# Four projections through the 512-column form, in halves of 256 output channels

## The chip, the cores and the metric

The kernel runs on one core of a Trainium2 chip. The metric is device time in microseconds (us), the median of repeated executions. Five engines work side by side, each through its own instructions in order: TensorE (PE, matmuls, with its weight loads PEld), VectorE (DVE), ScalarE (ACT), GpSimd (POOL) and SyncE (SP, here the queue that issues most loads).

## What is computed

One layer that mixes four branches: a gated linear recurrence, dilated window attention, an RWKV-7 recurrence and a convolution. All start from one product with a wide weight matrix (T is 256 tokens, D_MODEL 2048, D_IN 18048):

```
h = jnp.einsum('bsd,de->bse', x, w_in) + b_in
(a_x, a_gate, q, k, v, b_gate, c_r, c_k, c_v, c_wd, c_ad, c_gate,
 d_val, d_glu, d_gate, merge_logits) = jnp.split(h, split_points, axis=-1)
...
for n in range(N_BRANCH):
    mixed = mixed + merge_g[:, :, n] * jnp.einsum('bsc,cd->bsd', ys[n] * jax.nn.silu(gates[n]), w_br[n])
out = jnp.einsum('bsd,de->bse', mixed, w_out)
return _layernorm(ALPHA * x + out, ln_g, ln_b)
```

q and k have 1536 channels each and are read in three strips of 512; every gate has 512. The change touches four such strips of `w_in`: the gate of branch c, the first of q, the last of k, and the gate of branch b.

## The kernel before

**Precision.** Every factor of a large product is kept as a rounded part and a remainder: x as `xh` and `xl`, side by side in one tile `x2` (per row block 256 columns of `xh`, then 256 of `xl`), and the weights as `wh` (an ACT cast, L219) and `wl` (a DVE subtraction, shown at L65, which is the line of the wrapper through which all DVE work goes). A product is the sum of wh·xh, wh·xl and wl·xh, three matmuls.

**The two forms of a projection.** `proj` (L330, through `channel_major` and `multiply`, L240) gives 512 channels as four blocks of 128, each 256 columns wide, two blocks to a PSUM bank, so two banks for the whole projection; each of its 192 matmuls moves 256 columns. `wide` (L256) takes a whole bank for each block of 128 channels, moves `xh` and `xl` together as one operand of 512 columns against `wh` (L270), and `wl` against `xh` alone (L273); the two halves of the bank are added when the bank is emptied. It takes four banks: from the pool `pss` (four banks, the stream's) or from `psb` (four banks, shared with the recurrences and the attention). Of the six strips of q and k the four in the middle go through `wide`, the first of q (Q0 below) and the last of k (K2) through `proj`.

**What empties a bank.** For Q0 and K2 one ACT pass per block adds the bias (L977). For the gates, `silu_gate` (L333), one ACT sigmoid (L338) and one DVE pass per block. The gate of branch c is `gc`; it is then multiplied by `yc`, the result of the RWKV branch, and split into `ych` and `ycl` (`gated`, L342).

**What runs beside it.** The recurrences and the attention are generators that `pump` advances between weight pieces. Their DVE instructions are pinned behind everything already traced on DVE; the rest is placed by a scheduler that orders each engine's instructions before the run; splits of weights have a raised priority. The RWKV generator ends, for each of four chunks of 64 steps, with a chain: `bks` (DVE), transposes `pbk` (PE), `pu` (PE), `us` (DVE), `psa` (PE), `sv` (DVE copies), `pst` (PE), `sv` (DVE sums) and the next chunk's `pu`; after the last chunk `py` (PE), `wy` and its square `sq` (ACT), `psvar` (PE), `sel` (ACT square root), a reciprocal and two small splits into `selr` (DVE), `psvar` again (PE), then `wy` (DVE) and `yc` (DVE). In the program's text all of that is ahead of `gc` (`finish(yc)`, L966); on the engines the scheduler lays the matmuls of `gc` and Q0 between its steps.

**Rotation.** Tiles of one tag take turns: `pss` has 4 banks, `wh` and `wl` three buffers each, `raw` (the landed weights) four, `mg` two. A tile's first writer waits for the last reader of the tile that had the buffer.

Of the kernel before, what the change touches and what calls it, by code (L numbers as in the profile page):

```python
# [11 lines left out]
F32 = mybir.dt.float32  # L12
F32R = mybir.dt.float32r
AF = mybir.ActivationFunctionType
ALU = mybir.AluOpType
# [4 lines left out]
P = 128  # L20
T = 256
DM = 2048
KT = DM // P
KP = 2
BW = 512
NJ = BW // P
# [8 lines left out]
C_AX, C_AG, C_Q, C_K, C_V, C_BG = 0, 512, 1024, 2560, 4096, 5632  # L35
C_R, C_CK, C_CV, C_WA, C_CG = 6144, 6656, 7168, 7680, 7808
# [37 lines left out]
def tile_hybrid(  # L74
# [4 lines left out]
    S, G, PE = nc.scalar, nc.gpsimd, nc.tensor  # L79
    V = Paced(tc, nc.vector)  # L80
# [6 lines left out]
    bp = ctx.enter_context(tc.tile_pool(name="bp", bufs=1))  # L87
    pss = ctx.enter_context(tc.tile_pool(name="pss", bufs=4, space=PSUM))
# [3 lines left out]
    def big(tag, bufs, name, dt=F32):  # L92
        pool = ap if tag in ("mx4", "tt") else xp if tag in ("yh", "yl") else bp
        return pool.tile([P, NJ, T], dt, tag=tag, name=name, bufs=bufs)

    def tt(name, dt=F32):
        return big("tt", 5, name, dt)
# [4 lines left out]
    def ra(name, shape, dt=F32):  # L102
        return bp.tile(shape, dt, tag="ra", name=name, bufs=6)

    def bank(name):
        return psb.tile([P, 512], F32, tag="pb", name=name)
# [8 lines left out]
    x2 = xp.tile([P, KT, 2, T], F32R, tag="x2", name="x2")  # L115
    xh, xl = x2[:, :, 0, :], x2[:, :, 1, :]
# [5 lines left out]
    def load_x(k, n):  # L122
        xs = rk("xs")[:, 0:n, :]
        load(xs, xr[:, k : k + n, :])
        return xs

    def split_x(xs, k, n):
        V.tensor_copy(xh[:, k : k + n, :], xs)
        V.tensor_tensor(xl[:, k : k + n, :], xs, xh[:, k : k + n, :].bitcast(F32), op=ALU.subtract)
# [47 lines left out]
    def bcol(c):  # L177
        return bc[:, c // P : c // P + 1]
# [5 lines left out]
    def pump(budget):  # L184
        V.side = True
        credit[0] = min(credit[0], 0.0) + budget
        while side and credit[0] > 0:
            try:
                cost = next(side[0])
                credit[0] -= cost  # L190
            except StopIteration:
                side.popleft()
        V.side = False
# [9 lines left out]
    def fetch(src, c0, n, k, nk, queue=None):  # L203

        if nk == 1:
            raw = rk("raw1").rearrange("p a b -> p (a b)")[:, 0:n].rearrange("p (k n) -> p k n", k=1)
        else:
            raw = rp.tile([P, nk, n], F32, tag="raw", name="raw", bufs=4)
        ins = (queue or nc.sync).dma_start(raw, src[:, k : k + nk, c0 : c0 + n])
        if queue:  # L210
            tc.keep_in_program_order(ins)
        return raw

    def split(src, c0, n, k, nk, raw=None):
        raw = raw or fetch(src, c0, n, k, nk)
        h = wp.tile([P, nk, n], F32R, tag="wh", name="wh", bufs=3)
        l = wp.tile([P, nk, n], F32R, tag="wl", name="wl", bufs=3)
        with tc.high_priority(offset=AHEAD):
            S.copy(h, raw)  # L219
            V.tensor_tensor(l, raw, h.bitcast(F32), op=ALU.subtract)  # L220
        return h, l

    def pieces(nk, n):
        kn = KP * 512 // n
        return [(k, kn) for k in range(0, nk, kn)]

    w_in_r = w_in.rearrange("(k p) c -> p k c", p=P)
# [3 lines left out]
    def columns(n):  # L231
        ps = [pss.tile([P, 2, T], F32, tag="ps", name="ps") for _ in range((n // P + 1) // 2)]
        return [ps[j // 2][:, j % 2, :] for j in range(n // P)]

    def multiply(ps, h, l, k0, kn, nk, rh, rl, j0=0):
        for j in range(j0, len(ps)):
            for k in range(kn):
                kk = k0 + k
                for i, (w, r) in enumerate(((h, rh), (h, rl), (l, rh))):
                    PE.matmul(  # L240
                        ps[j],
                        w[:, k, (j - j0) * P : (j - j0 + 1) * P],
                        r[:, kk, :],
                        start=(kk == 0 and i == 0 and j % 2 == 0),
                        stop=(kk == nk - 1 and i == 2),
                        skip_group_check=True,
                    )
# [8 lines left out]
    def wide(c0, stream):  # L256

        ps = [pss.tile([P, 512], F32, tag="ps", name="ps") if stream else bank("psq") for _ in range(NJ)]
        for k0, kn in pieces(KT, 512):
            raw = fetch(w_in_r, c0, 512, k0, kn)  # L260
            h = [ra("wa", [P, 512], F32R) for _ in range(kn)]
            l = wp.tile([P, kn, 512], F32R, tag="wl", name="wl", bufs=3)
            with tc.high_priority(offset=AHEAD):
                for k in range(kn):
                    S.copy(h[k], raw[:, k, :])  # L265
                    V.tensor_tensor(l[:, k, :], raw[:, k, :], h[k].bitcast(F32), op=ALU.subtract)
            for j in range(NJ):
                for k in range(kn):
                    both = x2[:, k0 + k, :, :].rearrange("p a t -> p (a t)")
                    PE.matmul(ps[j], h[k][:, j * P : (j + 1) * P], both, start=(k0 + k == 0), stop=False, skip_group_check=True)  # L270
            for j in range(NJ):
                for k in range(kn):
                    PE.matmul(  # L273
                        ps[j][:, T:], l[:, k, j * P : (j + 1) * P], xh[:, k0 + k, :], start=False,
                        stop=(k0 + k == KT - 1), skip_group_check=True,
                    )
            pump(BUD)
        return ps

    def opening(cols, budget):  # L280

        pss_ = [columns(512) for _ in cols]
        todo = []
        for k0, kn in ((0, 1), (1, 1)) + tuple((k, KP) for k in range(2, KT, KP)):
            todo += [(k0, kn, n, q, T if k0 == 0 and n == 0 else 512) for n in range(2) for q in range(2 if k0 == 0 and n == 0 else 1)]

        def get(k0, kn, n, q, w):
            xs = load_x(k0, kn) if n == 0 and q == 0 else None
            return xs, fetch(w_in_r, cols[n] + q * w, w, k0, kn, S if kn == 1 and n == 0 else nc.sync)

        got = [get(*p) for p in todo[:5]]
        for i, (k0, kn, n, q, w) in enumerate(todo):
            if i >= len(got):
                got.append(get(*todo[i]))
            xs, raw = got[i]
            h, l = split(w_in_r, 0, w, k0, kn, raw)
            if xs is not None:
                split_x(xs, k0, kn)
            multiply(pss_[n][0 : 2 * q + w // P], h, l, k0, kn, KT, xh, xl, 2 * q)
            if n:  # L300
                pump(budget * kn)
        return pss_
# [25 lines left out]
    BUD = 1300.0  # L328

    def proj(c0, n=512):  # L330
        return channel_major(w_in_r, KT, c0, n, xh, xl, BUD)

    def silu_gate(c0, name):  # L333
        ps = proj(c0)
        g = tt(name)
        for j in range(NJ):
            b = bcol(c0 + j * P)
            S.activation(g[:, j, :], ps[j], AF.Sigmoid, bias=b)  # L338
            V.scalar_tensor_tensor(g[:, j, :], ps[j], b, g[:, j, :], op0=ALU.add, op1=ALU.mult)
        return g  # L340

    def gated(y, g, name):  # L342
# [593 lines left out]
    ps, pd = opening((C_AX, C_DL), BUD)  # L936
# [4 lines left out]
    ps = proj(C_DV)  # L941
# [7 lines left out]
    ps = proj(C_WA, 128)  # L949
# [14 lines left out]
    yhd = gated(yd[0], gd, "yd")  # L964
    merge(3, *yhd, False, False)
    finish(yc)  # L966
    gc = silu_gate(C_CG, "gc")
    yhc = gated(yc[0], gc, "yc")

    qk = []  # L970
    for i in range(6):
        c0 = C_Q + i * 512
        t = rk("qt" if i < 3 else "kt")
        pairs = 0 < i < 5
        ps = wide(c0, i % 2) if pairs else proj(c0)
        for j in range(NJ):
            S.activation(t[:, j, :], ps[j][:, T:] if pairs else ps[j], AF.Identity, bias=bcol(c0 + j * P))  # L977
            if pairs:
                V.tensor_tensor(t[:, j, :], t[:, j, :], ps[j][:, 0:T], op=ALU.add)
        qk.append(t)  # L980
    qt, kt = qk[0:3], qk[3:6]
    vt = []
    for g in range(3):
        bv = ra("bv", [P, 512])
        G.dma_start(bv, row(b_row[C_V + g * 512 : C_V + (g + 1) * 512]))
        ps = token_major(w_in_r, KT, C_V + g * 512, *by_token(xh, xl), BUD)
        t = rk("vt").rearrange("p a b -> p (a b)").rearrange("p (t n) -> p t n", t=2)
# [2 lines left out]
        vt.append(t)  # L990
    hb = bias_tiles()
    side.append(attention(qt, kt, vt, hb, yb))
    gb = silu_gate(C_BG, "gb")
    merge(2, *yhc, False, False)
    finish(yb)
    yhb = gated(yb[0], gb, "yb")
# [85 lines left out]
    for i, (c0, n) in enumerate(((0, 512), (512, 512), (1024, 512), (1536, 256))):  # L1082
        ps = token_major(w_out_r, KT, c0, mix(0), mix(1), BUD, n)
# [10 lines left out]
    for t in range(2):  # L1094
        ps = pss.tile([P, 512], F32, tag="ps", name="ps")
# [92 lines left out]
```

## Time and profile before

| | |
|---|---|
| median of 3 runs | 1047.32 us (1047.31 to 1048.41) |
| the profiled execution's own time | 1049.88 us |
| its span on the core | 1048.1 us |
| PE busy | 1039.7 us, 99% of the span |
| DVE, ACT busy | 729.3 us (70%), 501.2 us (48%) |
| granted TensorE clock, mean | 0.996 |

The rows come from one profiled execution; times in them are counted from the start of its span. A matmul in fp32 of small size shows as two records, and the ends of matmuls are modelled, so a row's duration runs a little past the start of the next one: the pace of a row of matmuls is read from start to start, or from the chain of waits, which gives each stretch without overlap. "Idle" is time in which an engine waited, and the name behind the arrow is what it waited for.

### The profile page before, as it was taken

To read this page: it belongs to the slowest core of one execution; us is meant where nothing else is said; L and a number is where in the kernel's file an instruction comes from. 1 tells how busy PE (TensorE), PEld (TensorE's weight loads), DVE (VectorE), ACT (ScalarE), POOL (GpSimd) and SP (SyncE) were. 2 spreads that over 40 slices of the span, in tenths; PEclk is the share of its full clock that TensorE was granted. 3 is DMA by queue.
4 is the path that set the end of the run, shared out by engine and by line. 5 is a ranking of instruction groups with operands and counts; after the bars stand their busy time and mean duration, and the time that the engine had idled before them with its cause. 6 is when DMAs were issued, how large, how long until landed. Compare 5 with 4: busy or idle time off the path is not lost.

```text
span 1048.1 us, 16209 instructions
## 1 busy us (share of the span) xinstructions
PE 1039.7 (99%) x6413; PEld 908.6 (87%) x6413; DVE 729.3 (70%) x1035; ACT 501.2 (48%) x628; POOL 31.7 (3%) x57
## 2 busy tenths in 40 slices
PE   9999999999999999999999999999999999999997
PEld 8999999887798878898888998898888888888886
DVE  6577989999996998654755444466666565556656
ACT  4456444457654444534545443346564444445341
POOL 0000000000011003000000200000000000000000
PEclk9999999999999999999999999999999999999998
DMA  9767666665566668544566786665556667666662
GB/s 310 226 195 233 193 186 191 191 203 179 170 180 191 198 188 240 165 126 134 165 195 184 246 269 196 188 184 155 173 155 211 206 200 220 206 200 223 191 188 95
DMA packets 109372, 203.07 MB, mean 194 GB/s; under 512 B 8468, under 2 KB 17600, under 8 KB 109296
## 3 DMA queue, kind: packets, MB, share of 16 engines
q1 hardware_dynamic: 104560, 189.25, 60.7%
q0 software_dynamic: 3584, 11.08, 3.4%
q10 hardware_dynamic: 1152, 1.70, 0.5%
q8 instruction: 50, 0.82, 0.3%
q14 instruction: 26, 0.21, 0.1%
HBM read 198.98 MB, written 5.39 MB: 195 GB/s over the span
## 4 chain that ended last, share of the span: by engine, by line
PE 89%; DVE 6%; DMA 3%; issue 2%; POOL 0%; ACT 0%; SPq 0%; POOLq 0%; DVEq 0%
PE ps L318 47%; PE ps L240 26%; PE ps L270 3%; PE psq L270 3%; DVE wl L65 3%; DVE xw L65 2%; PE psq L273 1%; PE ps L273 1%; DMA al<-scr 1%; PE psl L842 1%; DMA x<-scr 1%; PE ps L1098 1%; DVE z L65 1%; PE po L866 0%; DMA xs<-in_x_t 0%
## 5 line engine op out<-in xcount | busy, mean ns | idle before, releaser
L65 DVE TENSOR_TENSOR wl<-raw,wh 128x1024 fp32r<-128x1024 f32 (+1 forms) x313 | 378.8, 1212 | 222.9 <-ACT wh L219 219.4
L219 ACT CAST wh<-raw 128x1024 fp32r<-128x1024 f32 (+1 forms) x313 | 325.4, 1043 | 411.8 <-PE ps L318 236.5
L318 PE MATMUL ps<-wh,x 128*128 128x512 f32 x1216 | 356.5, 391 | 0.0
L240 PE MATMUL ps<-x,wh 128*128 128x256 f32 x1568 | 284.8, 285 | 0.0
L318 PEld LDWEIGHTS ps<-wh,x 128*128 128x128 f32 x1216 | 227.9, 188 | 46.3
L240 PEld LDWEIGHTS ps<-x,wh 128*128 128x128 f32 x1568 | 244.2, 192 | 2.3 <-issue 0.7
L318 PE MATMUL ps<-wl,x 128*128 128x512 f32 x608 | 220.4, 394 | 1.0 <-DVE wl L65 0.8
L240 PE MATMUL ps<-x,wl 128*128 128x256 f32 x784 | 221.0, 285 | 0.4 <-DVE wl L65 0.4
L240 PEld LDWEIGHTS ps<-x,wl 128*128 128x128 f32 x784 | 149.4, 192 | 1.3 <-DVE wl L65 0.8
L318 PEld LDWEIGHTS ps<-wl,x 128*128 128x128 f32 x608 | 114.2, 188 | 28.0 <-DVE wl L65 3.7
L318 PE MATMUL ps<-wh,m 128*128 128x512 f32 (+1 forms) x256 | 68.0, 364 | 0.0
L65 DVE TENSOR_TENSOR wl<-raw,wa 128x512 fp32r<-128x512 f32 x64 | 41.2, 688 | 37.4 <-ACT wa L265 32.9
L265 ACT CAST wa<-raw 128x512 fp32r<-128x512 f32 x64 | 36.3, 618 | 37.6 <-PE ps L270 18.9
L318 PEld LDWEIGHTS ps<-wh,m 128*128 128x128 f32 x256 | 45.9, 189 | 7.4
L65 DVE SCALAR_TENSOR_TENSOR acc<-cu,pkt,acc 128x256 f32<-128x256 f32 x120 | 51.1, 481 | 0.0
L318 PE MATMUL ps<-wl,m 128*128 128x512 f32 (+1 forms) x128 | 43.0, 364 | 0.0
L270 PE MATMUL ps<-x,wa 128*128 128x512 f32 x128 | 33.4, 393 | 0.0
L270 PE MATMUL psq<-x,wa 128*128 128x512 f32 x128 | 32.1, 393 | 0.0
L318 PEld LDWEIGHTS ps<-wl,m 128*128 128x128 f32 x128 | 24.1, 189 | 3.6
L270 PEld LDWEIGHTS psq<-x,wa 128*128 128x128 f32 x128 | 23.0, 189 | 4.1
L270 PEld LDWEIGHTS ps<-x,wa 128*128 128x128 f32 x128 | 22.5, 189 | 3.4
L887 ACT ACTIVATE mg<-mg 128x512 f32<-128x512 f32 x32 | 19.1, 628 | 10.2 <-DVE mg L65 10.2
(325 smaller groups left out, 939.9 us busy)
## 6 DMA issues: line engine op xcount, KB each, us to landing
raw<-in_w_in SPq DMA_DIRECT2D x280, 512.0 KB, 4.3
raw<-in_w_br SPq DMA_DIRECT2D x32, 512.0 KB, 4.7
raw<-in_w_out SPq DMA_DIRECT2D x32, 512.0 KB, 4.6
bm<-in_b_row SPq DMA_DIRECT2D x16, 256.0 KB, 5.1
fscr<-frow POOLq DMA_DIRECT2D x3, 768.0 KB, 7.8
z<-in_x POOLq DMA_DIRECT2D x4, 512.0 KB, 13.8
xs<-in_x_t SPq DMA_DIRECT2D x7, 256.0 KB, 5.3
hb<-fscr POOLq DMA_DIRECT2D x3, 512.0 KB, 9.2
```

Of the source, the lines that this page charges most:

```text
L65: ins = f(*a, **k)
L219: S.copy(h, raw)
L240: PE.matmul(ps[j], w[:, k, (j - j0) * P : (j - j0 + 1) * P], r[:, kk, :], start=(kk == 0 and i == 0 and j % 2 == 0), stop=(kk == nk - 1 an ...
L265: S.copy(h[k], raw[:, k, :])
L270: PE.matmul(ps[j], h[k][:, j * P : (j + 1) * P], both, start=(k0 + k == 0), stop=False, skip_group_check=True)
L273: PE.matmul(ps[j][:, T:], l[:, k, j * P : (j + 1) * P], xh[:, k0 + k, :], start=False, stop=(k0 + k == KT - 1), skip_group_check=True,)
L318: PE.matmul(ps[t][:, 0:n], a(kk, t), w[:, k, :], start=(kk == 0 and i == 0), stop=(kk == nk - 1 and i == 2),)
L842: PE.matmul(ps[:, 0:w], qt[g][:, h, q * P : (q + 1) * P], kt[g][:, h, 0:w], start=True, stop=True)
L887: S.activation(g, g, AF.Sigmoid)
L1098: PE.matmul(ps[:, 0:T], mix(a)(k, t), w[k // 4][:, k % 4, :], start=(k == 0 and i == 0), stop=(k == KT - 1 and i == 2))
```

## The change

`halved` is new: it gives the four blocks of a projection in two halves of 256 channels. Each half takes two banks of `pss`, runs over four weight pieces of 4 row blocks by 256 channels, and does in each piece 8 matmuls of 512 columns (wh against `xh` and `xl` together) and 8 of 256 (wl against `xh`). After a half its two banks are handed to whoever empties them. `silu_pairs` takes the place of `silu_gate` for `gc` and `gb`: per block an ACT pass with the bias on one half of the bank, a DVE sum with the other half, an ACT sigmoid into a tile of the tag `mg`, and a DVE product. Q0 and K2 also go through `halved`, and every strip of q and k is now emptied as `wide` is.

```
+    def halved(c0):
+        for q in range(2):
+            ps = [pss.tile([P, 512], F32, tag="ps", name="ps") for _ in range(2)]
+            for k0, kn in pieces(KT, T):
+                h, l = split(w_in_r, c0 + q * T, T, k0, kn)
+                for j in range(2):
+                    for k in range(kn):
+                        both = x2[:, k0 + k, :, :].rearrange("p a t -> p (a t)")
+                        PE.matmul(
+                            ps[j], h[:, k, j * P : (j + 1) * P], both, start=(k0 + k == 0), stop=False, skip_group_check=True
+                        )
+                for j in range(2):
+                    for k in range(kn):
+                        PE.matmul(
+                            ps[j][:, T:], l[:, k, j * P : (j + 1) * P], xh[:, k0 + k, :], start=False,
+                            stop=(k0 + k == KT - 1), skip_group_check=True,
+                        )
+                pump(BUD)
+            yield from ps
...
+    def silu_pairs(c0, name):
+        g = tt(name)
+        for j, ps in enumerate(halved(c0)):
+            S.activation(g[:, j, :], ps[:, T:], AF.Identity, bias=bcol(c0 + j * P))
+            V.tensor_tensor(g[:, j, :], g[:, j, :], ps[:, 0:T], op=ALU.add)
+            s = bp.tile([P, 512], F32, tag="mg", name="sg", bufs=2)[:, 0:T]
+            S.activation(s, g[:, j, :], AF.Sigmoid)
+            V.tensor_tensor(g[:, j, :], g[:, j, :], s, op=ALU.mult)
+        return g
...
-    gc = silu_gate(C_CG, "gc")
+    gc = silu_pairs(C_CG, "gc")
...
-        pairs = 0 < i < 5
-        ps = wide(c0, i % 2) if pairs else proj(c0)
-        for j in range(NJ):
-            S.activation(t[:, j, :], ps[j][:, T:] if pairs else ps[j], AF.Identity, bias=bcol(c0 + j * P))
-            if pairs:
-                V.tensor_tensor(t[:, j, :], t[:, j, :], ps[j][:, 0:T], op=ALU.add)
+        ps = wide(c0, i % 2) if 0 < i < 5 else halved(c0)
+        for j, p in enumerate(ps):
+            S.activation(t[:, j, :], p[:, T:], AF.Identity, bias=bcol(c0 + j * P))
+            V.tensor_tensor(t[:, j, :], t[:, j, :], p[:, 0:T], op=ALU.add)
...
-    gb = silu_gate(C_BG, "gb")
+    gb = silu_pairs(C_BG, "gb")
```

The scheduler lays the instructions of each engine anew. Three places matter below. **The first** is PE at the end of `gc`. Before, where `ps_4812` and `ps_4813` are the two banks of `gc`, `ps_5069` and `ps_5070` those of Q0, and `pu_4495` belongs to the last chunk of the RWKV chain:

```order
L240 MATMUL ps_4813<-x2_93,wl_5027 128x256
L240 MATMUL ps_5069<-x2_93,wh_5073 128x256 [waits Activation_49]
L240 MATMUL ps_5069<-x2_93,wh_5073 128x256
L240 MATMUL ps_5069<-x2_93,wl_5074 128x256
L240 MATMUL ps_5069<-x2_93,wh_5073 128x256 x2
L240 MATMUL ps_5069<-x2_93,wl_5074 128x256
L738 MATMUL pu_4495<-sv_4101,wt_3142 64x64 [waits DVE_49]
L240 MATMUL ps_5069<-x2_93,wh_5073 128x256
L738 MATMUL pu_4495<-sv_4101,wt_3142 64x64 [waits DVE_49]
```

Now, where `ps_4913` and `ps_4914` are the banks of the second half of `gc`, and `pu_4393` and `psa_4434` belong to the chunk before the last:

```order
L294 MATMUL ps_4913<-x2_93,wl_4984 128x256 x4
L294 MATMUL ps_4914<-x2_93,wl_4984 128x256 x4
L760 MATMUL pbk_4384<-cs_95,bks_4381 128x128 [waits DVE_49,PE_49]
L760 MATMUL pbk_4384<-cs_95,bks_4381 128x128 x3
L769 MATMUL pu_4393<-sv_4101,wt_3137 64x64 [waits PE_49]
L769 MATMUL pu_4393<-sv_4101,wt_3137 64x64 x7
L775 MATMUL py_4404<-wt_3137,sv_4101 64x64 [waits PE_49]
L775 MATMUL py_4404<-wt_3137,sv_4101 64x64 x7
L790 MATMUL psa_4434<-us_4402,xt_4014 64x64 [waits DVE_49,Activation_49]
```

Q0's matmuls, which stood between the steps of the last chunk, no longer do: the rest of that chunk, the whole last chunk and both `psvar` groups follow one another on PE.

**The second** is where Q0 begins. On PE before, the second `psvar` group stood in the middle of Q0's pieces:

```order
L240 MATMUL ps_5070<-x2_93,wl_5224 128x256
L509 MATMUL psvar_4656<-selr_4609 128x256 [waits DVE_49,PE_49]
L509 MATMUL psvar_4657<-selr_4609 128x256 [waits PE_49]
L240 MATMUL ps_5070<-x2_93,wh_5223 128x256 x2
L240 MATMUL ps_5070<-x2_93,wl_5224 128x256
L509 MATMUL psvar_4656<-selr_4609 128x256 [waits DVE_49]
```

Now Q0's first matmul (`ps_5019`) is the next one behind it, and waits for DVE:

```order
L524 MATMUL psvar_4611<-sq2_4579,cs_95 8x256 x3
L540 MATMUL psvar_4656<-selr_4609 128x256 [waits DVE_49,PE_49]
L540 MATMUL psvar_4657<-selr_4609 128x256 [waits PE_49]
L540 MATMUL psvar_4656<-selr_4609 128x256 [waits DVE_49]
L540 MATMUL psvar_4656<-selr_4609 128x256 x2
L540 MATMUL psvar_4657<-selr_4609 128x256 x3
L289 MATMUL ps_5019<-x2_93,wh_5023 128x512 [waits DVE_49]
```

`ps_5019` has the bank of `ps_4813`, the first block of `gc`. On DVE now its reader, the sum into `gc`, stands behind `yc`:

```order
L65 TENSOR_TENSOR wy_4176<-wy_4176,psvar_4656 128x512 [waits DMASW5_49,PE_49]
L65 TENSOR_TENSOR wy_4176<-wy_4176,psvar_4657 128x512 [waits PE_49]
L65 TENSOR_SCALAR wy_4176<-wy_4176,pkt_97 128x256 [waits DVE_49]
L65 TENSOR_SCALAR wy_4176<-wy_4176,pkt_97 128x256
L65 TENSOR_SCALAR wy_4176<-wy_4176,pkt_97 128x256 [waits DVE_49]
L65 TENSOR_SCALAR wy_4176<-wy_4176,pkt_97 128x256
L65 TENSOR_TENSOR yc_4690<-wy_4176,bn_2967 128x1024 [waits DVE_49]
L65 TENSOR_TENSOR gc_4812<-gc_4812,ps_4813 128x256 [waits Activation_49]
```

Before, `gc` was emptied behind `yc` too, but Q0 had banks of its own; now Q0 takes the banks of the first half of `gc`.

**The third** is PE at the end of `gb`, ahead of the third merge (its first bank is `ps_7253` before and `ps_7037` now; `pst`, `po` and `psl` are the attention's). Before, PE went from `gb` into the merge:

```order
L240 MATMUL ps_6874<-x2_93,wl_7185 128x256
L240 MATMUL ps_6874<-x2_93,wh_7184 128x256 x2
L240 MATMUL ps_6874<-x2_93,wl_7185 128x256
L318 MATMUL ps_7253<-wh_7257,x2_93 128x512 [waits Activation_49]
L318 MATMUL ps_7253<-wh_7257,x2_93 128x512
```

Now a whole step of the attention lies between, and the merge's first matmul waits for DVE:

```order
L294 MATMUL ps_6879<-x2_93,wl_6976 128x256 x4
L887 MATMUL pst0_6838<-cs_95,lg_6778 128x128 [waits DVE_49,Activation_49]
L887 MATMUL pst0_6838<-cs_95,lg_6778 128x128 x2
L892 MATMUL pst1_6843<-cs_95,lg_6778 128x128 x3
L897 MATMUL po_6848<-p0_6733,vt_6396 128x256 [waits Activation_49]
L897 MATMUL po_6848<-p0_6733,vt_6547 128x256
L897 MATMUL po_6848<-p0_6733,vt_6698 128x256
L873 MATMUL psl_6859<-kt_5633,qt_5018 128x128
L873 MATMUL psl_6862<-kt_5846,qt_5207 128x128 [waits PE_49]
L899 MATMUL po_6848<-p1_6734,vt_6396 128x128 [waits DVE_49]
```

The merge's first matmul stands five rows further on; its bank is that of the first block of `gb`, whose sum stands on DVE behind the maximum (`mx`) of the attention's next step.

## Rows read from the trace of the kernel before

**Rows 1.** The page's first part: busy time, share of span, instructions.

```profile
PE 1039.7 (99%) x6413; PEld 908.6 (87%) x6413; DVE 729.3 (70%) x1035; ACT 501.2 (48%) x628; POOL 31.7 (3%) x57
```

**Rows 2.** Chain of waits, 590 to 620: start, us, engine, tile, line, matmuls.

```profile
593.12 1.84 PE psq L270 x8
594.96 0.95 PE psq L273 x8
595.91 23.04 PE ps L240 x192
```

**Rows 3.** Stretch 461.50 to 506.35: busy us per engine, granted clock, DMA share.

```profile
461.50:506.35 44.85, 44.85 (x441) 41.17 (x440) 26.16 (x40) 21.63 (x32) 0.00 (x0) 1.00 0.45 130
```

**Rows 4.** DVE in order of time: start, us, instruction, idle before it.

```profile
463.58 1.23 DVE L65 TENSOR_TENSOR wl<-raw,wh 128x1024 fp32r<-128x1024 f32 x1 [0.93 <-ACT wh L219]
...
465.06 0.42 DVE L65 TENSOR_TENSOR bks<-kc,pc 128x256 f32<-128x256 f32 x1
466.20 0.42 DVE L65 COPY us<-pu 128x256 f32<-128x256 f32 x1 [0.72 <-PE pu L738]
...
469.62 0.87 DVE L65 COPY sv<-psa 64x256 f32<-64x256 f32 x2 [0.23 <-PE psa L759]
...
473.81 0.88 DVE L65 TENSOR_TENSOR sv<-pst,sd 64x256 f32<-64x256 f32 x2 [0.73 <-PE pst L769]
...
494.33 1.74 DVE L65 RECIPROCAL sel<-sel 8x256 f32<-8x256 f32 x1 [0.55 <-ACT sel L496]
...
496.42 0.41 DVE L65 TENSOR_TENSOR selr<-sel,selr 8x256 fp32r<-8x256 f32 x1
...
501.02 1.28 DVE L65 TENSOR_TENSOR wy<-wy,psvar 128x512 f32<-128x512 f32 x2
502.23 1.38 DVE L65 TENSOR_SCALAR wy<-wy,pkt 128x256 f32<-128x256 f32 x4
...
504.88 1.22 DVE L65 TENSOR_TENSOR yc<-wy,bn 128x1024 f32<-128x1024 f32 x1
```

**Rows 5.** ACT in order of time, the same columns.

```profile
487.18 0.37 ACT L779 COPY wy<-py 128x256 f32<-128x256 f32 x1 [1.92 <-PE py L775]
487.59 1.06 ACT L782 ACTIVATE sq<-wy 128x1024 f32<-128x1024 f32 x1
...
493.83 0.47 ACT L496 ACTIVATE sel<-psvar,eps_gn 8x256 f32<-8x256 f32 x1
...
500.44 0.84 ACT L338 ACTIVATE gc<-ps,bc 128x256 f32<-128x256 f32 x2
```

**Rows 6.** PE in order of time, the same columns.

```profile
468.90 0.68 PE L759 MATMUL psa<-us,xt 64*64 64x64 f32 x16
...
491.22 1.89 PE L493 MATMUL psvar<-sq,cs 128*8 128x256 f32 x8
...
499.59 0.97 PE L509 MATMUL psvar<-selr 8*128 8x256 f32 x6
```

**Rows 7.** The attention's step near `gb`: chain of waits, then one DVE row.

```profile
708.16 0.33 PE pst L856 x3
708.49 0.33 PE pst L861 x3
...
712.43 1.29 PE po L866 x6
713.73 0.67 PE po L868 x6
714.39 0.67 PE psl L842 x6
...
717.01 0.54 DVE L65 TENSOR_REDUCE mx<-lg 128x1 f32<-128x384 f32 x1
```

**Rows 8.** TensorE's clock: PE's first matmuls, then a stretch at the end.

```profile
1.19 4.02 PE L113 MATMUL idle<-zero 128*128 128x512 bf16 x9 [1.19 <-DVE zero L65]
...
1038.00:1040.00 2.00, 0.80 (x2) 0.01 (x1) 1.86 (x7) 0.29 (x1) 0.00 (x0) 0.89 0.35 131
```

## The prediction, made before the changed kernel had run

> **What bounds the kernel now.** I read the page's first part first: PE is busy in 1039.7 of 1048.1 us [rows 1], so whatever shortens or opens PE's row of matmuls moves the end, and everything else counts only where it makes PE wait. Then the chain of waits at the end of K, where both forms of a projection stand next to each other [rows 2]: eight 512-column matmuls take 1.84 us (230 ns each), eight of 256 columns 0.95 us (119 ns), and the 192 of `proj` 23.04 us (120 ns each). Last, because the order shows the rows near `gc` and `gb` moved, the same places in the trace: the stretch from the end of the second RWKV chunk to the end of Q0 [rows 3], the steps of the RWKV chain on DVE, ACT and PE [rows 4 to 6], and the attention's step near `gb` [rows 7]. In the stretch of rows 3 PE never rests: 44.85 of 44.85 us.
>
> **The saving, which is what the change is about.** A projection in halves has 8 pieces of 8 + 8 matmuls. From rows 2 a piece costs 1.84 + 0.95 = 2.79 us, and eight 22.3 us, against 23.04 us: 0.7 us a projection, 2.8 us for four. The row is of the same operands, the same x and fp32 form, so I take it without a margin. The Trainium skill (TensorE: Matmul & The Clock Gate, "Wait — 56ns, not 53.3ns?") gives a warm matmul a fixed cost of only about 2.5 ns over its columns; by that, 64 merged pairs would save 0.16 us a projection, some 0.6 us in all, and the sum below would come out 2.2 us longer. The rows above, 120 ns for 256 columns and 230 for 512, show about four times that fixed cost, and I go by them.
>
> **What is added and hidden.** A gate is now emptied by 8 ACT and 8 DVE passes instead of 4 and 4, Q0 and K2 by 4 more DVE passes each: at some 0.42 us (the short `us` copy, rows 4) 8 ACT and 16 DVE passes, 3.4 and 6.7 us. They are spread over four places, and DVE and ACT have work for 70% and 48% of the span [rows 1], so PE covers them, except for the one sum that PE waits for below. The 32 loads of `w_in` in 4 by 256 instead of 2 by 512 carry the same bytes in the same places of SP's queue; four buffers lie ahead of PE, and in the stretch of rows 3 the DMA engines are busy for only 0.45 of the time. I cost them at nothing; without that cover each late load would show as a wait of `wh` for a DMA.
>
> **What is added and not hidden: Q0 behind the RWKV chain.** `gc` used two banks, so that Q0 had the other two of `pss` and its 192 matmuls ran between the last chunks of the recurrence. In the trace ACT empties the first two blocks of `gc` only at 500.44 us [rows 5], behind `psvar` and `sel`, and nobody minds, since Q0 doesn't need them. In halves `gc` fills all four banks. Q0's first matmul needs the bank of the first block of `gc`, and the order puts the sum that frees it on DVE behind `yc`, the very end of the recurrence; `gc`'s last matmul is followed on PE by the rest of chunk 2, chunk 3 and `psvar`, with nothing in between. So PE now walks the chain at the pace of its links. Queued behind the waiting matmul are Q0 and all that follows.
>
> The links, from `gc`'s last matmul (which also frees the `wl` buffer that the next DVE split waits for):
> - split 1.23 us, then `bks` of chunk 3, from 463.58 to the end at 465.48: 1.9
> - `us` 0.42, `psa` 0.68, `sv` copies 0.87: 2.0
> - `pst`, as long as `psa`, 0.68, `sv` sums 0.88: 1.6
> - chunk 3: `pu` 0.5, `us` 0.42, `psa` 0.68, `sv` 0.87, last `py` 0.68: 3.2
> - `wy` 0.37, `sq` 1.06, `psvar` 1.89: 3.3
> - `sel` 0.47, then reciprocal and splits, from 494.33 to 496.83: 2.5; together 3.0 (the table load before `sel` runs beside `psvar`)
> - the second `psvar` group 0.97: 1.0
> - `wy` 1.28 and 1.38, `yc` 1.22, one sum 0.42: 4.3
>
> All from rows 4 to 6; `pu` is an estimate from `psa`. The sum is 20.3 us, and the chain has 14 handoffs between engines. An unqueued one within ACT can be seen where `sq` starts 0.04 us after `wy` ends [rows 5]; I take 0.1 us for each, as an estimate, so 21.7 us, with 20.3 (none) and 24 as ends. What the same steps cost PE before is in rows 3: of 44.85 us, 80 matmuls of `gc` and 192 of Q0 (counted in the order) took 272 times 120 ns, 32.6 us; the rest, 12.2 us, was the chain's own matmuls from the end of `pst` of chunk 1 on. They were paid before, so the loss is 21.7 - 12.2 = **+9.5 us**, with ends +8 and +12. Behind it Q0 finds three pieces already split, 8.4 us of work, while ACT and DVE finish `gc`; the fourth is split about a microsecond before it is needed, so I add nothing.
>
> **The merge behind `gb`.** The same happens there in small. The merge's first bank was free before; now it is that of the first block of `gb`, whose sum stands on DVE behind the maximum of the next attention step. From `gb`'s last matmul: transposes 0.66, a copy about 0.5, `po` and `psl` 2.63, one logit pass 0.25 (an estimate from the 0.54 of the maximum, which reads more), maximum 0.54, sum 0.42 [rows 7, 4]: 5.0 us. PE's own work in it, 0.33 + 0.33 + 1.29 + 0.67 + 0.67 = 3.3 us, was paid before. **+1.7 us**, between 0 and 4. K2 has no such place: two projections with banks elsewhere lie ahead of it and a whole strip of v behind.
>
> **TensorE's clock.** Before, PE never rested in the middle of the kernel, and the granted clock is 1.00 there. In the last microseconds PE is busy for 0.80 us of 2, and the granted clock falls to the lower of its two levels, 1.2 instead of 2.4 GHz (the mean of that stretch is 0.89) [rows 8]. In the new stretch PE works for some 10 of 22 us and rests for over 4 us ahead of Q0. So I expect the fall, and Q0's first matmuls at the lower level. What that costs is taken from the kernel's start, where nine matmuls of 512 columns at the lower level take 4.02 us, 447 ns each [rows 8]: against 230 ns [rows 2] they lose 2.0 us. Up to 6 us more come to it if all PE links of the chain (0.68 three times, 0.5, 1.89, 0.97) run at half pace as well. I take **+3.0 us** (Q0's start and a part of `psvar`), with 0 and 8 as ends. The Trainium skill (TensorE: Matmul & The Clock Gate, "What's actually happening") says that the throttled clock is the default state and activity releases it; the trace agrees at both ends of the kernel, and nothing in the sum comes from the page.
>
> **Sum.** -2.8 + 9.5 + 1.7 + 3.0 = +11.4 us against the profiled execution's 1049.88, so 1061.3 there with a span near 1059.5. The median was 2.56 us below the profiled execution; the same difference added to 1047.32 gives **1058.7 us**.
>
> **The rivals.**
> - *The chain is bare, the clock holds.* PE's small matmuls may be activity enough. For it: PE is never idle for long until the 4 us ahead of Q0. Against it: rows 8. -2.8 + 9.5 + 1.7 = +8.4: 1055.7.
> - *The clock is low through the whole chain, or the tail drags.* All links at half pace give +8 instead of +3: 1063.7, and somewhat more if the fourth piece of Q0 is late too.
> - *Not slower: the emptying of one half is covered by the other half's matmuls.* A half lasts four pieces, 11.2 us, and emptying two blocks needs about 2 us of ACT and DVE. If the chain is done before `gc`'s second half ends, only the saving is left, 1047.3 - 2.8 = 1044.5. It decides at a chain that ends 12 us earlier than I have it, at the time of `gc`'s last matmul. The Trainium skill (Perfetto Trace Analysis, "Matmuls") has this as a rule: independent groups of matmuls should rotate through different banks so that the emptying of one overlaps the next. Against it: in the trace `gc` was emptied from 500.44 us on, at least 17 us after its matmuls (Q0's 192, 23.0 us, end at 506.35), not 2 us after them, and DVE, which takes its instructions in order, has the sum behind `yc`.
> - *The pairs save nothing here* (more weight pieces are narrow, or each bank is reached in another way): 2.8 us on top of any of the first three; it is in the range, with no chance of its own.
>
> **How the numbers follow.** The forecast, chain bare and clock falling: 0.58, 1056 to 1062. Clock holds: 0.24. Low through the chain or a dragging tail: 0.13. Covered: 0.05. For 8 in 10 the range takes the low ends of the first two (1047.3 - 2.8 + 8 + 0 = 1052.5) and the third with half of its spread above (1064.5); only the covered case and the extremes are left out. What a measurement can tell from no change is about 0.2%, 2.1 us. Slower than that is every case with the bare chain save a few short ones: 0.93. The covered case is faster by 2.8 us: 0.04; within 0.2% is left 0.03.
>
> **What would show it.** In the profile after: PE's waits, some 8 us in all before, gain one of 4 to 5 us at the first matmul of `halved` on DVE's sum into `gc`, and several of 1 to 3 us at `psa`, `pst`, `py` and `psvar`; between `gc`'s last matmul and Q0's first lie 20 to 24 us. At the merge behind `gb` PE waits 1 to 2 us for DVE. A projection without other work takes 22.3 us (K2 shows it best). The granted clock is below 1.00 just before or at Q0's start. Wrong would be: Q0 starting within 12 us of `gc`'s end, waits of `wh` for a DMA in the four projections, or a K2 of 23 us.

## The result, and the profile after

The changed kernel takes 1063.44 us (median of 4 runs, 1061.76 to 1066.48), the kernel before 1047.87 beside it (4 runs, 1047.31 to 1049.54). The ratio is 1.0143, with a 95% interval of 1.0132 to 1.0155: 15.0 us slower. The forecast was 1058.7, with a range of 1052.5 to 1064.5. The profiled execution of the changed kernel has a span of 1062.3 us, 14.2 above the 1048.1 of before. Further down, two executions of e2b, one of e7 and one of the kernel before were slow (1275 us or more) and are in no time or ratio.

PE's busy time on the page of the changed kernel is the same as before to 0.1 us [rows 1]; its span is not. The second line is the new form's 512-column matmul (count, mean ns, idle time ahead of the group and who ended it), the third the granted clock in 40 slices:

```profile
PE 1039.8 (98%) x6157; PEld 896.9 (84%) x6157; DVE 734.1 (69%) x1051; ACT 502.0 (47%) x634; POOL 31.6 (3%) x57
...
L289 PE MATMUL ps<-x,wh 128*128 128x512 f32 x256 | 66.8, 401 | 3.7 <-DVE gc L65 3.7
...
PEclk9999999999999999996999999999999999999998
```

There are 256 matmuls fewer, but they were worth little, and a "busy" PE at a lower clock counts as busy too. PE's waits in the changed kernel (who waited, for whom, us in total, times, longest) name the places:

```profile
PE ps L289 <- DVE gc L65: 3.7, 1, 3.7
PE psvar L540 <- DVE selr L65: 2.7, 1, 2.7
PE psvar L524 <- ACT sq L813: 1.6, 1, 1.6
PE ps L339 <- DVE gb L65: 1.3, 1, 1.3
...
PE psa L790 <- DVE us L65: 1.1, 1, 1.1
```

The first three and the last lie in one stretch, behind `gc`. In the changed kernel's PE timeline (start, us, instruction, count, idle before it), with the chunk before in the first row, `gc`'s last matmuls in the second, and Q0's first in the second from the end:

```profile
466.16 0.68 PE L800 MATMUL pst<-sv,bk 128*64 128x64 f32 x14
...
470.01 1.12 PE L294 MATMUL ps<-x,wl 128*128 128x256 f32 x8
...
473.79 0.68 PE L790 MATMUL psa<-us,xt 64*64 64x64 f32 x16 [1.14 <-DVE us L65]
...
476.14 1.11 PE L800 MATMUL pst<-sv,bk 128*64 128x64 f32 x14
...
483.98 3.58 PE L524 MATMUL psvar<-sq,cs 128*8 128x256 f32 x8 [1.55 <-ACT sq L813]
490.30 2.04 PE L540 MATMUL psvar<-selr 8*128 8x256 f32 x8 [2.74 <-DVE selr L65]
496.00 2.08 PE L289 MATMUL ps<-x,wh 128*128 128x512 f32 x4 [3.66 <-DVE gc L65]
497.88 1.06 PE L294 MATMUL ps<-x,wl 128*128 128x256 f32 x4
```

Not one matmul of a projection stands between 470.97 and 496.00 us, 25.0 us, where before PE never rested [rows 3]. The same stretch in windows laid where the clock changes (length, then busy us of PE, PEld, DVE, ACT, POOL, then granted clock, DMA share, GB/s):

```profile
471.00:476.00 5.00, 3.26 (x62) 2.71 (x60) 3.91 (x8) 1.36 (x4) 0.00 (x0) 1.00 0.71 202
476.00:479.50 3.50, 3.50 (x53) 3.12 (x53) 0.84 (x2) 1.48 (x4) 0.00 (x0) 0.52 0.02 5
479.50:483.00 3.50, 2.18 (x47) 1.63 (x43) 1.69 (x4) 0.50 (x2) 0.00 (x0) 0.99 0.00 0
483.00:500.00 17.00, 9.62 (x27) 6.04 (x28) 10.26 (x19) 7.07 (x13) 0.00 (x0) 0.50 0.00 0
500.00:505.00 5.00, 5.00 (x29) 4.34 (x28) 2.45 (x2) 2.96 (x3) 0.00 (x0) 1.00 0.01 3
```

A mean of 0.50 is the lower level, 1.2 GHz, for a whole window. So the clock fell twice. The first time was just after 476 us, about 1 us after PE had come back from two waits of 1.1 and 0.6 us, and while it ran the chain's matmuls of 64 and 128 columns without a pause. By 479.5 us it was full again. The second time was at 483 us, in the wait ahead of the sum of squares, and it stayed low until 500 us. Its cost is in the durations above: `pst` 1.11 us where the same 14 matmuls take 0.68 in the chunk before, the sum of squares 3.58 where [rows 6] has 1.89.

Where the 14.2 us of span came from, from the starts of the same work in both traces:

| stretch | before | after | difference |
|---|---|---|---|
| start to `gc`'s first matmul (same program) | 440.90 | 441.91 | +1.0 |
| `gc` to Q0's last | 65.45 | 78.38 | +12.9 |
| K0 to Q2, the four wide ones | 89.40 | 89.42 | 0.0 |
| K2 alone | 23.04 | 22.35 | -0.7 |
| V | 66.12 | 66.13 | 0.0 |
| `gb` to merge(2)'s fourth strip | 145.72 | 147.06 | +1.3 |
| the rest | 217.47 | 217.05 | -0.4 |

The first row is not the change: among all kernels below, whose program is the same up to there but for one, that start lies between 438.6 and 441.9 us.

### The profile page after: what moved, and what is told of

The parts are those of the page before. It is cut to its first block, busy times and chain, and to the rows that moved or that the text cites. A ratio compares the mean times of both kernels' runs of the same rounds, so it can differ in the third digit from the quotient of the medians.

```text
span 1062.3 us, 15725 instructions
## 1 busy us (share of the span) xinstructions
PE 1039.8 (98%) x6157; PEld 896.9 (84%) x6157; DVE 734.1 (69%) x1051; ACT 502.0 (47%) x634; POOL 31.6 (3%) x57
## 4 chain that ended last, share of the span: by engine, by line
PE 90%; DVE 6%; DMA 2%; issue 1%; ACT 0%; POOL 0%; SPq 0%; DVEq 0%; POOLq 0%
PE ps L339 49%; PE ps L240 18%; PE ps L289 6%; PE ps L294 3%; PE ps L270 3%; PE psq L270 3%; DVE wl L65 2%; PE psq L273 1%; PE ps L273 1%; DVE xw L65 1%; DVE z L65 1%; PE psl L873 1%; DMA x<-scr 1%; PE ps L1127 1%; PE po L897 1%
## 5 line engine op out<-in xcount | busy, mean ns | idle before, releaser
L240 PE MATMUL ps<-x,wh 128*128 128x256 f32 x1056 | 190.5, 284 | 0.0
L240 PEld LDWEIGHTS ps<-x,wh 128*128 128x128 f32 x1056 | 164.0, 192 | 1.0 <-ACT wh L219 0.3
L240 PE MATMUL ps<-x,wl 128*128 128x256 f32 x528 | 147.9, 284 | 0.8 <-DVE wl L65 0.8
L240 PEld LDWEIGHTS ps<-x,wl 128*128 128x128 f32 x528 | 100.3, 192 | 1.5 <-DVE wl L65 1.2
L289 PE MATMUL ps<-x,wh 128*128 128x512 f32 x256 | 66.8, 401 | 3.7 <-DVE gc L65 3.7
L289 PEld LDWEIGHTS ps<-x,wh 128*128 128x128 f32 x256 | 46.8, 193 | 12.3 <-DVE gc L65 4.0
L294 PEld LDWEIGHTS ps<-x,wl 128*128 128x128 f32 x256 | 35.8, 192 | 3.0
L294 PE MATMUL ps<-x,wl 128*128 128x256 f32 x256 | 37.3, 286 | 0.0
```

Of the source, the lines that this page charges most:

```text
L240: PE.matmul(ps[j], w[:, k, (j - j0) * P : (j - j0 + 1) * P], r[:, kk, :], start=(kk == 0 and i == 0 and j % 2 == 0), stop=(kk == nk - 1 an ...
L289: PE.matmul(ps[j], h[:, k, j * P : (j + 1) * P], both, start=(k0 + k == 0), stop=False, skip_group_check=True)
L294: PE.matmul(ps[j][:, T:], l[:, k, j * P : (j + 1) * P], xh[:, k0 + k, :], start=False, stop=(k0 + k == KT - 1), skip_group_check=True,)
```

## The experiments

In all of them "the changed kernel" is the one predicted, and the edit is against it unless it says otherwise. Times are medians; ratios are against the kernel before in the same runs.

**What holds the emptying back.** The prediction read from the order that `gc`'s emptying stands behind the chain's end, and asked no further. In the timeline of ACT, after the change, the first pass over `gc`'s banks follows `sel` at once, although the first two banks were full about 15 us before `gc`'s last matmul:

```profile
487.60 0.46 ACT L527 ACTIVATE sel<-psvar,eps_gn 8x256 f32<-8x256 f32 x1 [2.37 <-PE psvar L524]
487.97 1.52 ACT L366 ACTIVATE gc<-ps,bc 128x256 f32<-128x256 f32 x4
```

and on DVE, in the same view, the sums follow `yc`:

```profile
494.39 1.22 DVE L65 TENSOR_TENSOR yc<-wy,bn 128x1024 f32<-128x1024 f32 x1
495.53 1.41 DVE L65 TENSOR_TENSOR gc<-gc,ps 128x256 f32<-128x256 f32 x4
```

ACT rested for 2.37 us ahead of `sel`, so it is no full queue. In the order of instructions, raising the priority of these passes, by up to 6000 places, changes nothing on any engine; writing the first pass into a scratch tile of another tag moves that pass of the first block ahead of `sel`, while the sum into `gc` stays behind `yc`. (These are orders of instructions; they were not run.) What binds is the *tile* `gc`. It is one of five buffers of the tag `tt`, as `yc` is; in the program's text `yc` is written first, and nothing that writes into `gc` is placed before the write of `yc`. (Why the scheduler has it so was not looked into; asking for `gc`'s tile earlier in the text does not change it.) The same holds at `gb`, whose writes come behind those of `yb` in the attention. So the next three kernels take `yc` and `yb` out of those buffers.

**e1: `yc` in place.**

```diff
-        yc = tt("yc")
+        yc = wy
         V.tensor_tensor(yc, wy, bn, op=ALU.add)
```

> The changed kernel with one line altered: the chain's result yc is written into the tile of wy and takes no tile of its own of the five (tag tt) from which the gate gc gets its tile too; in its order of instructions the emptying of gc's banks now stands ahead of the chain's last steps. Theory 1 (what costs is PE bare behind the chain, because gc's four banks are emptied late): Q0 starts within 1 us of gc's last matmul, the wait on gc's sums (3.7 us in the changed kernel) and the lower clock at 480 to 500 us are gone, and the stretch from gc's first to Q0's last matmul falls from 78.5 us to about 64 (65.5 in the kernel before, less two times 0.7); in all the kernel before less four times 0.7 plus the 1.3 us at gb: 1046.4 us, 1045 to 1048. Rival (the paired form itself costs: its additional passes on ScalarE and VectorE hold the chain's steps up wherever they stand): the chain gets longer by the 4 to 5 us of passes between its steps, and Q0 or K0 pays for it: 1050 to 1056 us.

1046.88 us (11 runs); ratio 0.9992 (0.9984 to 1.0001), some 16 us below the changed kernel. In its timelines, ACT's first pass over `gc` comes in the middle of `gc`'s matmuls, and the second pass for the other half right behind them:

```profile
453.22 0.84 ACT L366 ACTIVATE gc<-ps,bc 128x256 f32<-128x256 f32 x2
...
468.85 0.83 ACT L366 ACTIVATE gc<-ps,bc 128x256 f32<-128x256 f32 x2
```

On PE, K0's first matmul, where Q0 is done, comes 61.5 us after `gc`'s first (439.60) instead of 78.4:

```profile
501.12 0.70 PE L270 MATMUL ps<-x,wa 128*128 128x512 f32 x2 [0.48 <-DVE qt L65]
```

Theory 1 holds, its rival does not: the additional passes between the chain's steps cost nothing that can be seen. The stretch is 2.5 us shorter than the 64 us expected; about 1.5 of that is the second `psvar` group, which now lies in K0 (at 507.77 us) and not ahead of it, and the rest no run ties to a place.

**e2: `yb` in place as well.**

```diff
-        y = tt("yb")
+        y = qt[0]
```

> As e1_yc_inplace, and the attention's result yb is written into the tile of the first queries, so that gb's tile is not handed out behind it either. Theory 1: gb's banks are emptied during its own projection, merge(2) starts without the 1.3 us wait on gb's sums: 1045.1 us, 1044 to 1047, and 1.3 us below e1_yc_inplace. Rival (merge(2) would wait for the attention's steps anyway, as in the kernel before): same time as e1_yc_inplace within 0.5 us.

1046.26 us (11 runs); ratio 0.9975 (0.9963 to 0.9987). This version beats both kernels. Against e1 it gains 0.6 us by the medians and 1.8 by the ratios, so the times alone hardly tell the theory from its rival; the traces do: from `gb`'s first matmul to merge(2)'s fourth strip it is 147.08 us in e1 (680.77 to 827.85) and 145.06 in e2 (681.26 to 826.32), 2.0 less. Once more, beside e8:

> e2_both_inplace once more on another day's chip, beside e8: theory 1 puts it 0.7 us below e8_all_but_gc_inplace, 1045 to 1047, 0.1 to 0.4% faster than the kernel before; rival: within 0.1% of the kernel before, and its first measurement was the chip's mood.

1046.41 us (10 runs), ratio 0.9976 (0.9965 to 0.9988): 2.5 us below the kernel before, where the four savings alone are 2.8. In the changed kernel `gb` was emptied only when the attention had copied its first head into `yb`, and merge(2) waited for it. ACT in the changed kernel, then PE:

```profile
725.89 0.37 ACT L900 COPY yb<-po 128x256 f32<-128x256 f32 x1 [2.77 <-PE po L899]
726.16 1.57 ACT L366 ACTIVATE gb<-ps,bc 128x256 f32<-128x256 f32 x4
```

```profile
727.38 0.73 PE L339 MATMUL ps<-wh,x 128*128 128x512 f32 x2 [1.30 <-DVE gb L65]
```

In e2, on PE, the same matmul follows `gb`'s last without a wait:

```profile
704.27 1.12 PE L294 MATMUL ps<-x,wl 128*128 128x256 f32 x8
705.22 0.63 PE L339 MATMUL ps<-wh,x 128*128 128x512 f32 x2
```

**e3: the two lines in the kernel before.**

> The kernel before with the same two results in place (yc in wy, yb in the first queries), its four projections as they were. Theory 1: in the kernel before nothing waited for the gates' banks, since a projection there takes two of the four, so emptying them sooner is worth nothing: the kernel before within 0.2%, 1046 to 1049 us. Rival (the two lines are a gain by themselves, whatever the form of the projections): 1 to 3 us below the kernel before.

1048.10 us (11 runs), ratio 1.0003 (0.9994 to 1.0011). The two lines are worth nothing by themselves; here they pay only where a projection goes through all four banks.

**e4: idle matmuls in the bare stretch.** 34 in all, each set at a place in the text by a line like the third:

```diff
+    def spin(t, n):
+        for _ in range(n):
+            PE.matmul(t, xh[:, 0, 0:P], x2[:, 0, :, :].rearrange("p a t -> p (a t)"), start=True, stop=True)
...
             S.activation(r8, ps[0:8, 0:T], AF.Sqrt, bias=eps[0:8], scale=scale)
+            spin(ps, 9)
```

> The changed kernel with 34 idle matmuls of 512 columns (operands: the first chunk of x) put where PE waits between gc and Q0: 5 and 2 in the third chunk of the chain, 4 ahead of the sum of squares, 9 behind it, 14 behind the scaling, each set into a bank that the chain has just left; their results are overwritten. Theory 1 (part of the bare stretch is the lower clock): granted clock of at least 0.9 at 480 to 500 us instead of 0.65 and 0.50, the sums of squares of 3.6 us back at 1.9, Q0's first pieces at 1.8 us instead of about 3, in all 4 to 6 us less than the changed kernel: 1058 to 1060 us. Rival (the stretch is hand-overs between engines, and the low clock hides in their waits): within 1 us of the changed kernel, or up to 2 us above it, where the idle matmuls stand in the way.

1057.73 us (4 runs), ratio 1.0093 (1.0079 to 1.0107): 5.7 us less than the changed kernel's median (5.2 by the ratios), although PE has more to do. In its windows the clock holds:

```profile
470.00:480.00 10.00, 8.84 (x144) 6.96 (x141) 5.65 (x14) 2.84 (x8) 0.00 (x0) 1.00 0.23 71
480.00:490.00 10.00, 9.02 (x41) 5.97 (x40) 5.97 (x10) 5.17 (x8) 0.00 (x0) 1.00 0.00 0
490.00:500.00 10.00, 10.00 (x56) 8.40 (x55) 8.35 (x14) 5.71 (x8) 0.00 (x0) 1.00 0.09 18
```

and in its PE timeline the chain's links and Q0's start are at full pace (the row at 490.66 starts Q0; `gc`'s last matmul ended at 468.89):

```profile
472.32 0.68 PE L799 MATMUL psa<-us,xt 64*64 64x64 f32 x16
...
480.80 1.89 PE L528 MATMUL psvar<-sq,cs 128*8 128x256 f32 x8
483.25 2.35 PE L110 MATMUL psvar<-x 128*128 128x512 f32 x9 [0.56 <-ACT sel L531]
485.52 1.23 PE L545 MATMUL psvar<-selr 8*128 8x256 f32 x8
...
490.66 1.19 PE L293 MATMUL ps<-x,wh 128*128 128x512 f32 x4
```

From `gc`'s last to Q0's first matmul it is 21.8 us instead of 25.0, from `gc`'s first to Q0's last 73.29 (439.83 to 513.12) instead of 78.38. So at least **5.1 us** of the stretch were clock: 1.1 in the chain up to the sum of squares, 2.2 from there to Q0, 1.8 in Q0. What is left, 73.29 - 65.45 + 2 x 0.7 = 9.2 us, is the bare chain at full clock. The idle matmuls themselves hold the chain up a little: `psa` starts 3.43 us after `gc`'s last matmul (472.32 - 468.89), in the changed kernel 2.82 (473.79 - 470.97). Without these 0.6 us the split would be about 5.7 of clock and 8.6 of bare chain, as an estimate. The Trainium skill (TensorE: Matmul & The Clock Gate, "What's actually happening") has activity release a throttled default; the two sets of windows agree, 0.50 beside 1.00 for the same chain, with only the idle matmuls between them.

**e5: `gc` alone in the new form**, Q0, K2 and `gb` as before.

> Of the four projections only gc in the new form; Q0, K2 and gb as in the kernel before. Theory 1 (gc's four banks, emptied late, are the whole loss): Q0 waits at its first matmul for gc's sums although it is in the old form; the stretch from gc's first matmul to Q0's last is the changed kernel's 78.4 us plus 0.7 for Q0 in the old form, K2 0.7 more, gb and merge(2) 0.6 less: the changed kernel plus about 0.7 us, 1063 to 1065. Rival (Q0 in halves, with two banks in each, is what blocks): within 0.3% of the kernel before, 1045 to 1051.

1060.97 us (5 runs), ratio 1.0104 (1.0082 to 1.0126): most of the loss from one of the four projections. Q0 in the old form waits in the same place for the same 3.7 us, and `gc`'s first to Q0's last matmul is 78.76 us (440.91 to 519.67), 79.1 expected. The size of the total is a partial miss: the loss is 10.9 us by the ratio (8.6 to 13.2) where 15.7 was expected. Between the two profiled executions the difference is only 1.5 us, 1.0 of it ahead of `gc`, where the programs are equal; the rest no run ties to a place. The five runs spread over 4.2 us, and the two shortest (1058.6 and 1059.1) have the highest mean granted clock, 0.993 and 0.991, the two longest (1062.8) 0.989 and 0.988: how much the clock falls seems to differ between executions, but only one of them has a trace.

**e6: all but `gc` in the new form.**

> gc as in the kernel before, Q0, K2 and gb in the new form. Theory 1: gc leaves two banks free, Q0's first half takes them and empties them itself for its second half, all behind no step of the chain; the chain stays covered, three times 0.7 us are saved and 1.3 lost at merge(2): 1047.2 us, 1046 to 1048.5. Rival (Q0 in halves blocks by itself): PE is bare for some 10 us of the chain: 1056 to 1063.

1054.57 us (5 runs), ratio 1.0051 (1.0033 to 1.0069). Both theories miss; this one I had not seen. `gc` in the old form leaves two banks, but it keeps its own two until behind `yc`, and Q0 in halves needs the other two twice. Its second half waits for the sums of its first, and K0, which takes all four, for the sums of the second, which stand on DVE behind `yc` and two of `gc`'s. The two waits in PE's timeline:

```profile
492.80 1.20 PE L289 MATMUL ps<-x,wh 128*128 128x512 f32 x4 [1.56 <-DVE qt L65]
...
508.92 1.22 PE L270 MATMUL ps<-x,wa 128*128 128x512 f32 x2 [2.96 <-DVE qt L65]
```

In the second and behind it the clock is at its lower level for a while, as two windows show:

```profile
500.00:510.00 10.00, 7.04 (x40) 6.00 (x40) 9.59 (x20) 2.81 (x7) 0.00 (x0) 0.90 0.58 175
510.00:520.00 10.00, 10.00 (x47) 8.69 (x46) 5.02 (x6) 3.92 (x7) 0.00 (x0) 0.76 0.13 42
```

**e8: the same with `yc` and `yb` in place**, to see whether the banks are the reason.

> e6_all_but_gc with yc and yb in place as in e2_both_inplace: gc in the old form, Q0, K2 and gb in the new, every gate emptied as soon as its banks are full. Theory 1 (what e6_all_but_gc lost, 4.6 us of waits on the sums of Q0 and some 3 us of lower clock behind them, came from gc still holding two of the four banks): both waits shrink to under 1 us, the clock stays at 1.00, three times 0.7 us are saved: 1046.0 us, 1045 to 1047.5. Rival (Q0 in halves waits for its own banks whatever gc does, since it needs two of them twice): the waits on the sums of Q0 stay at 3 to 4.6 us: 1050 to 1054.

1047.89 us (12 runs), ratio 0.9992 (0.9983 to 1.0001). Both waits are gone, and PE and its clock are full:

```profile
490.00:500.00 10.00, 10.00 (x55) 7.51 (x54) 3.31 (x5) 7.57 (x12) 0.00 (x0) 1.00 0.48 149
500.00:510.00 10.00, 10.00 (x57) 8.28 (x56) 9.25 (x18) 1.06 (x3) 0.00 (x0) 1.00 0.51 157
```

So it was `gc`'s late emptying there too. In time it is 1.5 us above e2b where 0.7 was expected, and its gain of three savings on the kernel before, 2.1 us, shows only as 0.8, at the edge of what the interval can tell. On the core the gain is there: the median span of its runs is 1044.8 us, against 1047.3 for the kernel before and 1044.6 for e2b. What differs is the time outside the span, 3.2 us in the median where the other two have 1.8; why, no run shows.

**e7: the gates `ga` and `gd` in the new form, on top of e2.**

> e2_both_inplace with the gates ga and gd in the new form as well. Theory 1 (a projection saves 0.7 us wherever its banks are emptied in time): 1.4 us below e2_both_inplace, some 1044.9 us. Rival (ga and gd lie where VectorE is 87 to 95% busy, and their two additional passes of 0.35 us for each 128 channels go straight into the time, 4 to 5 us for both): equal to e2_both_inplace or up to 3 us above it, 1046 to 1049.5.

1049.33 us (10 runs), ratio 1.0001 (0.9989 to 1.0013). The rival has the time: 2.6 us above e2 by the ratios. Its reason is not what the traces show. `ga`, where DVE is busy for 95% of the time, takes 22.34 us (156.42 to 178.76) for e2's 23.04, and PE waits for nothing there: the 0.7 us are saved. The loss is at `gd`, from whose first matmul to `gc`'s first it is 146.87 us for e2's 143.37. The new form has an ACT pass (the sigmoid) behind a DVE sum, and DVE rests ahead of the last sum for 6.74 us, until a DMA into `al` has landed (2.64 us in e2). So ACT's sigmoid comes late, the next cast of weights behind it too, and PE waits. DVE, ACT twice, then PE:

```profile
332.61 0.42 DVE L65 TENSOR_TENSOR gd<-gd,ps 128x256 f32<-128x256 f32 x1 [6.74 <-DMA al<-scr]
```

```profile
333.06 0.42 ACT L369 ACTIVATE sg<-gd 128x256 f32<-128x256 f32 x1 [6.74 <-DVE gd L65]
333.38 1.03 ACT L219 CAST wh<-raw 128x1024 fp32r<-128x1024 f32 x1
```

```profile
334.47 1.90 PE L339 MATMUL ps<-wh,x 128*128 128x512 f32 x4 [2.13 <-ACT wh L219]
```

In 330 to 340 us PE is busy for 7.76 us of 10 at a granted clock of 0.83; in e2 PE never rests there and the clock is 1.00. So here too the price lies in where the emptying stands, and not in how much there is of it.

## Why the prediction was right, and where it was off

The forecast was +11.4 us in all; the ratio says +15.0 and the two traces +14.2, of which 1.0 lies ahead of all that was changed. By its own steps:

- **The saving, -0.7 us a projection: right.** In the changed kernel K2 runs from 609.71 to 632.06 us, with no other work in it: 22.35 us for the 23.04 of [rows 2], forecast 22.3. By an estimate from the fixed cost of some 2.5 ns that the Trainium skill gives (TensorE: Matmul & The Clock Gate, "Wait — 56ns, not 53.3ns?") the saving would be 0.16 us, so 22.9; the measurement decides for the rows.

```profile
609.71 1.55 PE L289 MATMUL ps<-x,wh 128*128 128x512 f32 x6
...
632.06 0.63 PE L339 MATMUL ps<-wh,x 128*128 128x512 f32 x2
```

- **The additional passes and the narrower loads at nothing: right in the changed kernel, but with little to spare.** e2 leaves 2.6 and 2.5 us of the 2.8 saved. A split did wait for a DMA, which the prediction named as a sign of being wrong: in K2 of the changed kernel ACT rests for 6.33 us ahead of one cast (2.9 at most in the kernel before), and PE is not held up. In K2 of e2 it is, for 0.72 us, by the cast behind such a load (0.43 in e2b, 0.19 in e8, 1.42 in e7). At `gd` the same assumption would have been wrong (e7). ACT in the changed kernel, then PE in e2:

```profile
621.97 1.05 ACT L219 CAST wh<-raw 128x1024 fp32r<-128x1024 f32 x1 [6.33 <-DMA raw<-in_w_in]
```

```profile
609.44 2.11 PE L289 MATMUL ps<-x,wh 128*128 128x512 f32 x8 [0.72 <-ACT wh L219]
```

- **Q0 behind the chain, +9.5 us: right.** The chain added up from the rows of before gave 21.7 us from `gc`'s last to Q0's first matmul; e4, at full clock, has 21.8 (21.2 without the hold-up of its idle matmuls), and the loss is 9.2 us (8.6). In the changed kernel itself the distance is 25.0, outside the 20 to 24 announced, because the sum of links was made at full clock and the clock is not full.
- **TensorE's clock, +3.0 us: the term that was mis-sized.** It measured 5.1 or a little more (e4 against the changed kernel), inside its ends of 0 and 8. Q0's start was right: 2.0 us forecast, 1.8 measured (its first twelve matmuls take 4.3 us for 2.4). What was too small is the chain's part. The prediction gave it 1 us, "a part of `psvar`". The rows show 2.2 us from the start of the sum of squares to Q0 (12.02 us for 9.86 in e4; both `psvar` groups are slow, 3.58 for 1.89 and 2.04 for 1.23), and at least 1.1 us ahead of that, from the first fall just after 476 us, which the prediction did not have: PE was running the chain's small matmuls one behind the other there (`pst` 1.11 for 0.68). The rival with the clock low through the whole chain has this part, but between 479.5 and 483 us the clock was full. The price also came from a doubtful place: the prediction took the kernel's start for the lower level, from a pace of 447 ns for 512 columns [rows 8], while the granted clock of the kernel before reads 1.00 there (row below); why the two differ no run shows. The changed kernel has the price with its clock beside it: Q0's first four matmuls of 512 columns take 470 ns each (496.00 to 497.88) at 0.50.

```profile
2.00:4.00 2.00, 2.00 (x6) 0.75 (x5) 0.62 (x2) 1.69 (x2) 0.00 (x0) 1.00 0.99 306
```

- **The merge behind `gb`, +1.7 us: right, 2.0 measured.** PE waits for 1.30 us; the stretch is 1.3 us longer although `gb` itself is 0.7 shorter in it, and e2, without the wait, has it 2.0 shorter than e1.
- **Why `gc` is emptied late: read rightly, explained by the wrong thing.** The order did have the sum behind `yc`, and the prediction gave DVE's taking its instructions in order as the reason. Its consequence held for this kernel. But an order has a cause, here that both tiles come from one tag's buffers, and two lines that nobody reads as part of a schedule move it (e1, e2). The third rival, emptying covered by the other half, was put at a chain that would have to end 12 us earlier; in e2 it came true with the chain later, not earlier (`yc` starts at 513.6 us, before at 504.9), and with 2.6 us of gain for the 2.8 forecast.

Added up, -2.8 + 9.2 + 2.0 + 5.1 = +13.5 us; the traces have 13.2 from `gc`'s first matmul on, with 0.4 less in the rest of the table. The rest of the measured 15.0 is the 1.0 us ahead of `gc` in that trace and 0.8 by which the ratio and the two profiled executions differ; no run ties it to a place. The measured 1063.44 lies near the upper end of the range, which the prediction had put there for a lower clock. Of the 3.6 us missing from its +11.4, the clock is 2.1, and the 1.0 and the 0.8 belong to no step of it; that they still fell inside the range is luck.

## What to carry to other kernels

When a change lets a stage take more of a pool of banks, look first at when the stage ahead of it gives its banks back, and not only at the order in which that stands but at what fixes the order: here the output tile of a gate came from the same small set of buffers as the end of a long recurrence. Where a chain of small steps may become bare, sum its links twice, at full and at half clock. How busy an engine is on average does not tell whether a saving on PE will last: `ga` kept its 0.7 us with DVE busy for 95%, and `gd` lost more than that to one sum that stood behind a DMA (e7).

## What the runs showed of the hardware that was not expected

- TensorE's granted clock fell while PE was busy: it was 1.00 until 476 us and 0.52 from there to 479.5, with PE busy throughout, after waits of 1.1 and 0.6 us, and with nothing but the chain's small matmuls in it. Before, the same matmuls stood between those of `gc` and Q0, at 1.00 [rows 3].
- A lower clock does not show in PE's busy time as a loss: 1039.7 and 1039.8 us in two kernels whose spans differ by 14.2 us.
- In e4, 34 matmuls that compute nothing, 9.1 us of PE's time (1.42 + 0.63 + 1.19 + 2.35 + 3.51), took 5 to 6 us off the kernel: they lie in PE's waits, and the chain's sum of squares behind them takes 1.89 instead of 3.58 us.
